# The attention's pass for the largest scores: high part of the queries alone, one shared maximum over the last keys

## Chip, cores and metric

The kernel runs on one core of one Trainium2 chip. The metric is the time of one execution on the device in microseconds; of several executions the median counts.

## The reference, cut to what matters

Two layers of a diffusion backbone over 1024 latent tokens of width 1024, with 256 context tokens. The change lies in layer 0, whose mixer runs grouped-query attention beside a bidirectional mLSTM. The attention has 8 query heads of 64, two key/value heads, 1280 keys (256 of context, 1024 latent):

```python
s = jnp.einsum('bhgtd,bhsd->bhgts', qblk, kt).astype(jnp.float32) * scale
p = jax.nn.softmax(s, axis=-1).astype(vt.dtype)
return jnp.einsum('bhgts,bhsd->bhgtd', p, vt)
```

The output projection, an expert-choice mixture of 16 experts, and a second layer (pooling mixer, 16 experts again) follow.

## The kernel before, in words

Matmuls that need float32 accuracy are made of float32r parts: a value is split into a high part and a low part, each exact in float32r, and a product is the sum of three products of parts.

*Layout.* For a head the queries stand along the free dimension, 1024 of them, in two tiles. QA has the high part of the 64 channels twice (partitions 0 to 63 and 64 to 127). QB has the low part in partitions 0 to 63, zeros below, and in row 64, once it is known, the negated largest score of each query. For the keys, KS has the high part over the low part, and K2 the high part over a row of ones (row 64) and zeros. So QA times KS is the queries' high part times the whole keys, and QB times K2 is the queries' low part times the keys' high part, plus the number in row 64. One product after the other into the same place gives a score with its query's largest score taken off.

*The pass for the largest scores* is `largest(h)`, a generator. For each of 8 tiles of 128 queries it makes three tiles of scores in PSUM (keys 0 to 511, 512 to 1023, 1024 to 1279), each with two matmuls (lines 648 and 649), and VectorE takes the maximum along the keys (line 650): 24 steps per head. At its end VectorE takes the maximum over the three blocks (653), TensorE transposes (655), ScalarE copies (657), the row goes to DRAM from the SP queue (659) and from there into row 64 of QB from the POOL queue (660). `queries(h)` fills QA and QB; ScalarE writes QA, VectorE the low part.

*The pass for the output* is `weighted(h)`: in 20 iterations (two halves of the queries, ten tiles of 128 keys) two matmuls (683, 684) make scores with the keys along the partitions, ScalarE takes the exponential (686) and its high part (57), VectorE the low part (58, for head 7 692 and 693), and three matmuls (695 to 697) add into the output and the sum. 684 is the matmul that reads QB with row 64 filled.

*Order.* `largest(0)` is stepped inside layer 0's projections, five steps of the attention's start per token tile, its score tiles in the projections' PSUM pool `tr` with three places. For heads 0 to 6, while `weighted(h)` runs, `largest(h + 1)` is stepped twice in iterations 0, 1, 2 of each five and once in the two others; one step of the mLSTM follows each five. The mLSTM has 24 steps, so it ends during head 5 or 6. Score tiles of `largest` have two places in PSUM here (`sc`), those of `weighted` two (`se`). The framework decides, when the program is built, in which order each engine's queue holds its instructions, with the program's order as priority; each engine then runs its queue in order, and waits on semaphores.

Of the kernel before, what the change touches and what calls it, by code (L numbers as in the profile page):

```python
# [11 lines left out]
F32 = mybir.dt.float32  # L12
# [6 lines left out]
AX = mybir.AxisListType.X  # L19
PSUM = bass.MemoryType.PSUM  # L20
# [5 lines left out]
NT = 8            # latent token tiles  # L26
NTA = 10          # context + latent token tiles
KB = 8            # blocks of 128 along the model width
# [4 lines left out]
ORDER = (3, 2, 1, 0)      # layer 1's groups of channels, the last ones first  # L33
# [3 lines left out]
def bc(ap, n=128):  # L37
    """rows of a DRAM vector for n partitions"""
    return bass.AP(tensor=ap.tensor, offset=ap.offset, ap=[[0, n]] + [list(e) for e in ap.ap][-1:])


class Kern:
# [5 lines left out]
    # ---------------------------------------------------------------- helpers  # L48
# [6 lines left out]
    def split(self, hi, lo, src):  # L55
        """src = hi + lo, each of them exact in float32r"""
        self.nc.scalar.copy(hi, src)  # L57
        return self.nc.vector.tensor_tensor(lo, src, hi.bitcast(F32), op=ALU.subtract).ins  # L58

    def rstd(self, pool, ss, n, tag, power=False):  # L60
        """1/sqrt(ss/n + eps) of a [p, m] tile of sums: a power on GpSimd, or exp(-ln/2) and one Newton step"""
# [20 lines left out]
    def staged(self, shape, name="raw", slot=None):  # L82
        """one of two 8 KB places for what comes from DRAM, in turns"""
        if slot is None:
            self.turn = 1 - self.turn
            slot = self.turn
        return self.raw.tile(shape, F32, name=name, tag=f"raw{slot}")

    def quarters(self, src):
        """two float32r parts of an 8 KB tile [128, KB, 256], each in two tiles of four blocks"""  # L90
# [8 lines left out]
    def load_half(self, w, k0, c0, n, extra=None):  # L99
        """rows k0*128.. of four blocks and columns c0..c0+n of w; two pairs of blocks, each in two float32r parts"""  # L100
# [15 lines left out]
    def table(self, name):  # L116
        """from here on ScalarE's functions come from this set"""
# [6 lines left out]
    # ---------------------------------------------------------------- constants  # L124
    def consts(self, pool, tmp, psp):
# [9 lines left out]
        # vectors that are wanted along the partitions: rows, then one transpose  # L135
# [28 lines left out]
    def mixer_consts(self, pool, tmp):  # L164
        """masks of the scans' two directions, and the matrix that reverses a chunk"""
# [13 lines left out]
    def choice_consts(self, pool, tmp):  # L179
        """for the choice of tokens: partitions are (token tile, expert)"""  # L180
# [30 lines left out]
    # ---------------------------------------------------------------- adaLN  # L211
    def mod0(self, pool, work, pp, tr, hp):
        """shift and scale of layer 0 for latent and context, as columns"""
# [29 lines left out]
    def mod_steps(self, xp, work, psp):  # L243
        """the other rows of the latent stream's modulation, in small steps: to DRAM, or for a norm's first two to columns"""
# [41 lines left out]
    # ---------------------------------------------------------------- layer 0, norm and projections  # L286
    def norm_transpose(self, xp, hp, sp, psp, srcs, dst, a, s, act=()):
        """two token tiles -> modulated rmsnorm, transposed, in two float32r parts; dst(j) -> (hh, hl) of blocks j, j + 1"""
# [29 lines left out]
    def layer0_proj(self, early):  # L318
# [3 lines left out]
        with ExitStack() as es:  # L322
# [24 lines left out]
            def hb(t, k):  # L347
                """stationary operands of token tile t (two of context, then latent), block k"""
# [8 lines left out]
            # rotary tables times the head norms' weights (q also times the scale of the scores)  # L357
# [20 lines left out]
            def headnorm(ps, nh, which, t, dst):  # L378
                """rmsnorm of nh heads of 64 and the rotation (latent tiles), into dst"""
# [132 lines left out]
    def gates(self, psp, pool):  # L512
        """the scalars of the mLSTM: rows are (chunk, direction, head), time runs along them, reversed for backward"""
# [64 lines left out]
        # M and the weight of the state along the free dimension, in the order of the tokens  # L578
# [7 lines left out]
    # ---------------------------------------------------------------- layer 0, attention and mLSTM  # L586
    def attention_start(self, es, psp):
        """keys and values of both kv heads, and the first head's queries with their largest scores"""
# [30 lines left out]
    def queries(self, h):  # L619
        """queries of head h along the free dimension: the high part twice; the low part over zeros"""  # L620
# [17 lines left out]
    def largest(self, h):  # L638
        """the largest score of each query of head h, negated, as a row of QB"""
        nc, sp = self.nc, self.qs  # L640
        QA, QB = self.Q[h]
        mx = sp.tile([128, NT, 3], F32, name="mx", tag="mx")
        for t in range(NT):
            ts = slice(t * 128, (t + 1) * 128)
            for b, (c0, c1) in enumerate(((0, 512), (512, 1024), (1024, 1280))):
                ps = self.sc[0].tile([128, 512], F32, name=self.sc[1], tag=self.sc[1])
                o = ps[:, :c1 - c0]
                nc.tensor.matmul(o, QA[:, ts], self.KS[h // 4][:, c0:c1], start=True, stop=False)
                nc.tensor.matmul(o, QB[:, ts], self.K2[h // 4][:, c0:c1], start=False, stop=True)
                nc.vector.reduce_max(mx[:, t, b:b + 1], o, axis=AX)  # L650
                yield
# [10 lines left out]
    def mixers(self):  # L662
        tc, nc, I = self.tc, self.nc, self.I
        KS, K2, VA, VL, Q = self.KS, self.K2, self.VA, self.VL, self.Q
        with ExitStack() as es:
# [7 lines left out]
            def weighted(h):  # L673
                """exp(scores - largest), keys along the partitions, times the values; over the sum"""
# [32 lines left out]
            for h in range(8):  # L707
# [4 lines left out]
                for i, _ in enumerate(weighted(h)):  # L712
                    for _ in range(2 if i % 5 < 3 else 1):
                        next(nxt, None)
                    if i % 5 == 4:
                        next(M, None)
# [9 lines left out]
    def mlstm_steps(self, pool, psp):  # L726
        """both scans, the context's two chunks first; a chunk's output when both directions have been there"""
# [12 lines left out]
    def mlstm(self, pool, psp, d, c):  # L740
# [18 lines left out]
        # what both directions share: the keys by position, and keys times queries  # L759
# [59 lines left out]
    def mlstm_out(self, pool, psp, c):  # L819
        """head norm and output gate of a latent chunk, transposed to channels"""  # L820
# [19 lines left out]
    # ---------------------------------------------------------------- second half of a layer: norm, router, choice  # L840
    def norm2_load(self, l, rows, wr, tmp):
        """the vectors of a layer's second half; rows: tiles for its scale and shift"""
# [8 lines left out]
    def norm2_setup(self, l, n2, xt, nj, st, pst, psl):  # L851
        """pools of a layer's second half. The router takes the stream itself: the norm's weight goes into the
        router's, its shift into a constant"""
# [17 lines left out]
    def half(self, t, x1, c):  # L871
        """half of the columns of a token tile of the stream: its squares' sum, and the channels along the partitions"""
# [10 lines left out]
    def logits(self, t, c, start, stop):  # L883
        """the router's product with half of the channels of a token tile"""
# [5 lines left out]
    def norm2(self, t, x1):  # L890
        """x1 of a token tile -> DRAM; 1/rms"""
# [7 lines left out]
    def store(self, dst, t, src, pairs):  # L899
        """a token tile to DRAM, or two of them that lie together"""  # L900
# [5 lines left out]
    def normed(self, t, x1, r):  # L906
        """the modulated norm of a token tile -> DRAM"""
# [18 lines left out]
    def router(self, t, c, r):  # L926
        """the affinities of a token tile, with half c of the channels still to come"""
# [12 lines left out]
    def topk(self, p, pools):  # L940
        """per expert the 128 tokens of largest affinity, the lower token first among equals: each token's slot, or none.
        The 128th largest comes digit by digit, two bits at a time: as floats of one sign order like their bits"""
# [69 lines left out]
        # the affinities in three exact parts  # L1012
# [6 lines left out]
    def wo_piece(self, i):  # L1019
        """a quarter of the output projection: half of the rows, half of the columns"""  # L1020
# [6 lines left out]
    def R(self, i, shape, dt=F32R):  # L1027
        """one of the 8 KB places"""
# [3 lines left out]
    def out0(self):  # L1032
        """output projection of layer 0, residual, then the second half's preparation"""
# [69 lines left out]
    # ---------------------------------------------------------------- experts  # L1103
    def moe(self, l, last=False):
        tc, nc, I = self.tc, self.nc, self.I
        with ExitStack() as es:
# [37 lines left out]
            def turned(src, nm):  # L1144
                """[slot, 1024] -> transposed blocks in two float32r parts"""
# [18 lines left out]
            def choose(e):  # L1164
                """token numbers and gates of an expert's slots, picked by products with ones and zeros"""
# [34 lines left out]
            for e in range(16):  # L1200
# [32 lines left out]
                if e == 15:  # L1233
                    # the stream after 15 experts; the last one's rows come by a product with ones and zeros
# [21 lines left out]
            def rows(t):  # L1256
                """the last expert's rows, onto x in PSUM or in SBUF, in turns"""
# [45 lines left out]
            def scale(x):  # L1303
                """1/rms"""
# [15 lines left out]
    # ---------------------------------------------------------------- layer 1  # L1320
    def w_raw(self, i):
        """a group's columns of layer 1's projection"""
# [4 lines left out]
    def w_normed(self, raw, out, t, engine):  # L1327
        """the norm's weight in w_raw(i); the norm's shift times it, summed over the blocks"""
# [11 lines left out]
    def w_shift(self, s1):  # L1340
        """the shift's way through the weights, one number per channel"""
# [7 lines left out]
    def layer1(self):  # L1349
        tc, nc, I = self.tc, self.nc, self.I  # L1350
        LO = [w // 2 for w in (2, 4, 8, 16)]
        with ExitStack() as es:
# [5 lines left out]
            # 1/count of the clipped windows at both ends  # L1358
# [15 lines left out]
            # the channel scales of the mixer and of its way into the stream  # L1374
# [7 lines left out]
            def invariants():  # L1382
                """1/rms of the tokens along the free axis"""
# [9 lines left out]
            def channels(i, between=iter(())):  # L1393
                """u of a group, its window means minus u, in two parts; the group's weights"""
# [27 lines left out]
                for m in range(2):  # L1422
                    # u with zeros on both sides, then windows of doubling width
# [35 lines left out]
            def done_half():  # L1459
                """the columns of the first two groups, while the last one is under way"""  # L1460
# [143 lines left out]
```

## Time and profile before

| what | us |
|---|---|
| median of 3 runs | 2348.63 |
| lowest, highest run | 2342.78, 2350.05 |
| span of the profiled execution, first to last instruction | 2342.2 |
| the profiled execution's own time beside its span | not shown by any view |
| `largest(0)`, inside the projections | 353 to 379 |
| attention with mLSTM, `weighted` of heads 0 to 7 | 391 to 751 |

The span comes from one profiled execution, the runs from others. Lines named PE are TensorE matmuls, PEld its weight loads, DVE VectorE, ACT ScalarE, POOL GpSimd, SP the sync engine; a q behind the name marks the engine's sequencer, which issues transfers. A duration of a matmul includes its way through the pipeline, so that consecutive ones overlap.

### The profile page before, as it was taken

How to read it: one execution, taken by the hardware profiler on the slowest of the kernel's cores; microseconds unless marked ns; L12 is line 12 of the kernel's file. 1: busy time of each engine (PE TensorE's matmuls, PEld its weight loads, DVE VectorE, ACT ScalarE, POOL GpSimd, SP SyncE). 2: the span in 40 equal slices, each digit the busy share in tenths (PEclk: the TensorE clock that was granted, in tenths of full speed). 3: DMA queues.
4: the chain of work that ended last, by engine and by line, in shares of the span. 5: the costliest groups of instructions: out<-in, count | busy, mean ns of one | idle time of the engine just before them, and what ended most of it. 6: DMA issues, size and time to landing. Idle time of an engine off the chain costs nothing.

```text
span 2342.2 us, 30036 instructions
## 1 busy us (share of the span) xinstructions
PE 2164.1 (92%) x10531; PEld 1729.5 (74%) x10531; DVE 1982.6 (85%) x3075; ACT 1406.1 (60%) x1994; POOL 259.3 (11%) x369
## 2 busy tenths in 40 slices
PE   6889999999998984999999999889749999999997
PEld 3768887787675863788888887578637888888875
DVE  7887754889997548999999998886789999999986
ACT  6413223667785223777777777522337777777774
POOL 0111120000000020000000010550300000000001
PEclk9899999999999996999999999999869999999999
DMA  7576753233423656999999996322849999999974
GB/s 271 197 248 231 257 176 99 66 109 89 111 76 113 226 203 258 355 381 394 380 385 387 380 386 227 99 73 88 335 177 358 389 383 378 391 384 378 394 250 153
DMA packets 206636, 599.42 MB, mean 256 GB/s; under 512 B 16708, under 2 KB 60180, under 8 KB 205460
## 3 DMA queue, kind: packets, MB, share of 16 engines
q1 hardware_dynamic: 168480, 481.81, 54.3%
q0 software_dynamic: 20704, 74.49, 10.9%
q10 hardware_dynamic: 17300, 41.20, 4.9%
q8 instruction: 83, 1.36, 0.2%
q14 instruction: 69, 0.57, 0.1%
HBM read 544.87 MB, written 52.58 MB: 255 GB/s over the span
## 4 chain that ended last, share of the span: by engine, by line
PE 77%; DVE 11%; ACT 4%; DMA 4%; issue 3%; POOL 1%; ACTq 0%; POOLq 0%; DVEq 0%; SPq 0%
PE u L51 6%; PE u L52 6%; PE u L53 6%; PE g L53 5%; PE g L52 5%; PE g L51 5%; PE d L52 5%; PE d L53 5%; PE d L51 5%; PE pp L51 3%; PE pp L52 3%; PE pp L53 3%; PE tr L1151 2%; DVE wl L58 2%; PE y L51 2%
## 5 line engine op out<-in xcount | busy, mean ns | idle before, releaser
L58 DVE TENSOR_TENSOR wl<-R,wh 128x1024 fp32r<-128x1024 f32 x512 | 614.4, 1236 | 39.2 <-ACT wh L57 36.7
L57 ACT CAST wh<-R 128x1024 fp32r<-128x1024 f32 x512 | 534.1, 1052 | 173.1 <-PE d L53 56.5
L58 DVE TENSOR_TENSOR wl<-X,wh 128x1024 fp32r<-128x1024 f32 x178 | 211.0, 1219 | 13.9 <-ACT wh L57 13.1
L57 ACT CAST wh<-X 128x1024 fp32r<-128x1024 f32 x178 | 186.0, 1050 | 54.8 <-PE d L53 22.8
L52 PE MATMUL d<-wl,ah 128*128 128x512 f32 x512 | 203.8, 398 | 5.5 <-DVE wl L58 5.5
L51 PE MATMUL d<-wh,ah 128*128 128x512 f32 x512 | 205.1, 400 | 2.9 <-DVE o L1186 2.9
L51 PE MATMUL g<-wh,xh 128*128 128x512 f32 x512 | 206.1, 402 | 1.5 <-ACT xh L57 1.5
L52 PE MATMUL g<-wl,xh 128*128 128x512 f32 x512 | 203.1, 397 | 1.8 <-DVE wl L58 1.8
L51 PE MATMUL u<-wh,xh 128*128 128x512 f32 x512 | 204.4, 399 | 0.0
L52 PE MATMUL u<-wl,xh 128*128 128x512 f32 x512 | 202.6, 396 | 0.6 <-DVE wl L58 0.6
L53 PE MATMUL g<-wh,xl 128*128 128x512 f32 x512 | 203.2, 397 | 0.0
L53 PE MATMUL d<-wh,al 128*128 128x512 f32 x512 | 202.8, 396 | 0.0
L53 PE MATMUL u<-wh,xl 128*128 128x512 f32 x512 | 202.1, 395 | 0.0
L57 ACT CAST wh<-raw 128x1024 fp32r<-128x1024 f32 (+1 forms) x112 | 115.5, 1037 | 56.8 <-PE pp L53 13.9
L58 DVE TENSOR_TENSOR wl<-raw,wh 128x1024 fp32r<-128x1024 f32 (+1 forms) x112 | 131.7, 1202 | 14.0 <-ACT wh L57 13.0
L686 ACT ACTIVATE e<-se 128x512 f32<-128x512 f32 x160 | 93.3, 595 | 65.2 <-PE se L684 49.9
L52 PEld LDWEIGHTS d<-wl,ah 128*128 128x128 f32 x512 | 96.8, 189 | 29.8 <-DVE wl L58 8.9
L51 PEld LDWEIGHTS d<-wh,ah 128*128 128x128 f32 x512 | 96.9, 189 | 25.1 <-ACT ah L57 3.8
L52 PEld LDWEIGHTS g<-wl,xh 128*128 128x128 f32 x512 | 97.2, 190 | 23.8 <-DVE wl L58 2.7
L51 PEld LDWEIGHTS g<-wh,xh 128*128 128x128 f32 x512 | 97.1, 190 | 23.6 <-ACT xh L57 2.5
L52 PEld LDWEIGHTS u<-wl,xh 128*128 128x128 f32 x512 | 96.4, 188 | 23.2 <-DVE wl L58 1.9
L53 PEld LDWEIGHTS d<-wh,al 128*128 128x128 f32 x512 | 96.8, 189 | 22.7 <-DVE al L58 0.5
(559 smaller groups left out, 4944.9 us busy)
## 6 DMA issues: line engine op xcount, KB each, us to landing
R<-in_w_exp_gate SPq DMA_DIRECT2D x87, 1024.0 KB
R<-in_w_exp_down SPq DMA_DIRECT2D x85, 1024.0 KB
R<-in_w_exp_up SPq DMA_DIRECT2D x79, 1024.0 KB
wm<-in_w_mod POOLq DMA_DIRECT2D x80, 512.0 KB, 5.3
X<-in_w_exp_up SPq DMA_DIRECT2D x33, 1024.0 KB
X<-in_w_exp_down SPq DMA_DIRECT2D x30, 1024.0 KB
X<-in_w_exp_gate SPq DMA_DIRECT2D x26, 1024.0 KB
raw<-in_w_exp_up SPq DMA_DIRECT2D x16, 1024.0 KB
```

The lines of the kernel that those rows point to most:

```text
L51: mm(ps, lh, rh, start=start, stop=False)
L52: mm(ps, lh, rl, start=False, stop=False)
L53: self.mark = mm(ps, ll, rh, start=False, stop=stop).ins
L57: self.nc.scalar.copy(hi, src)
L58: return self.nc.vector.tensor_tensor(lo, src, hi.bitcast(F32), op=ALU.subtract).ins
L686: nc.scalar.activation(e, ps, AF.Exp)
L1151: nc.tensor.transpose(ps[:, j * 128:(j + 1) * 128], src[:, (4 * q + j) * 128:(4 * q + j + 1) * 128], self.idf)
```

## The change

The matmul with the queries' low part is left out of `largest`, so that the number found is the largest product of the high part alone. What is subtracted from a score before the exponential is common to numerator and sum. The first two blocks of keys keep a PSUM tile each per tile of queries. For the last 256 keys, two tiles of queries share one PSUM tile, and one reduction gives both maxima. There are 20 steps per head instead of 24, and `mixers` takes them in another rhythm: two in iteration 0 of each five, one in the four others. The diff also strips comments and docstrings, which is left out here.

```diff
     def largest(self, h):
         nc, sp = self.nc, self.qs
         QA, QB = self.Q[h]
+        KS = self.KS[h // 4]
         mx = sp.tile([128, NT, 3], F32, name="mx", tag="mx")
-        for t in range(NT):
-            ts = slice(t * 128, (t + 1) * 128)
-            for b, (c0, c1) in enumerate(((0, 512), (512, 1024), (1024, 1280))):
-                ps = self.sc[0].tile([128, 512], F32, name=self.sc[1], tag=self.sc[1])
-                o = ps[:, :c1 - c0]
-                nc.tensor.matmul(o, QA[:, ts], self.KS[h // 4][:, c0:c1], start=True, stop=False)
-                nc.tensor.matmul(o, QB[:, ts], self.K2[h // 4][:, c0:c1], start=False, stop=True)
-                nc.vector.reduce_max(mx[:, t, b:b + 1], o, axis=AX)
-                yield
+        PS = lambda: self.sc[0].tile([128, 512], F32, name=self.sc[1], tag=self.sc[1])
+        for t in range(0, NT, 2):
+            for i in range(2):
+                for b in range(2):
+                    ps = PS()
+                    nc.tensor.matmul(ps, QA[:, (t + i) * 128:(t + i + 1) * 128], KS[:, b * 512:(b + 1) * 512],
+                                     start=True, stop=True)
+                    nc.vector.reduce_max(mx[:, t + i, b:b + 1], ps, axis=AX)
+                    yield
+            ps = PS().rearrange("p (i k) -> p i k", i=2)
+            for i in range(2):
+                nc.tensor.matmul(ps[:, i], QA[:, (t + i) * 128:(t + i + 1) * 128], KS[:, 1024:1280], start=True, stop=True)
+            nc.vector.reduce_max(mx[:, t:t + 2, 2], ps, axis=AX)
+            yield
         m8 = sp.tile([128, NT], F32, name="m8", tag="m8")
...
                 for i, _ in enumerate(weighted(h)):
-                    for _ in range(2 if i % 5 < 3 else 1):
+                    for _ in range(2 if i % 5 == 0 else 1):
                         next(nxt, None)
```

## Rows read from the trace of the kernel before

**Rows 1.** The page: span; busy time, share and instructions of two engines.
```profile
span 2342.2 us, 30036 instructions
...
PE 2164.1 (92%) x10531; PEld 1729.5 (74%) x10531; DVE 1982.6 (85%) x3075; ACT 1406.1 (60%) x1994; POOL 259.3 (11%) x369
```

**Rows 2.** Window of `largest(0)`: busy us per engine; then its matmuls by form, 348 to 391.
```profile
353.40:379.30 25.90, 25.90 (x121) 21.16 (x120) 14.34 (x27) 3.76 (x7) 0.00 (x0) 1.00 0.10 38
...
L648 PE MATMUL tr<-KS,QA 128*128 128x512 f32 x16 | 6.5, 406 | 0.0
L649 PE MATMUL tr<-K,QB 128*128 128x512 f32 x16 | 6.3, 394 | 0.0
```

**Rows 3.** Windows by head: PE, PEld, DVE, ACT, POOL busy (count), clock, DMA.
```profile
391.10:435.70 44.60, 41.70 (x200) 30.81 (x199) 36.02 (x72) 31.22 (x59) 2.80 (x9) 0.96 0.38 117
435.70:486.40 50.70, 50.35 (x284) 39.58 (x282) 43.63 (x95) 35.08 (x74) 1.76 (x5) 1.00 0.29 88
486.40:537.70 51.30, 51.18 (x302) 42.26 (x300) 46.09 (x105) 36.96 (x83) 1.85 (x6) 1.00 0.39 113
537.70:582.20 44.50, 43.47 (x233) 33.82 (x231) 41.24 (x100) 31.64 (x74) 1.75 (x5) 1.00 0.29 78
582.20:626.80 44.60, 40.69 (x203) 29.58 (x201) 41.54 (x104) 33.75 (x92) 1.16 (x3) 1.00 0.40 104
626.80:678.70 51.90, 48.85 (x264) 38.40 (x264) 49.33 (x129) 40.25 (x107) 2.13 (x5) 1.00 0.25 74
678.70:715.00 36.30, 33.97 (x155) 24.55 (x152) 33.72 (x64) 32.17 (x62) 0.00 (x0) 1.00 0.36 116
715.00:751.30 36.30, 30.93 (x110) 18.33 (x110) 28.64 (x53) 18.21 (x30) 1.32 (x8) 0.95 0.31 98
```

**Rows 4.** Timeline in head 1: start, duration, instruction; 512 columns, then 256.
```profile
452.02 0.39 PE L648 MATMUL sc<-KS,QA 128*128 128x512 f32 x1
...
452.25 0.39 PE L649 MATMUL sc<-K,QB 128*128 128x512 f32 x1
...
453.00 0.28 PE L648 MATMUL sc<-KS,QA 128*128 128x256 f32 x1
...
453.12 0.28 PE L649 MATMUL sc<-K,QB 128*128 128x256 f32 x1
```

**Rows 5.** VectorE's groups by form, 391 to 751: busy, mean ns, idle before.
```profile
L650 DVE TENSOR_REDUCE mx<-sc 128x1 f32<-128x512 f32 x112 | 75.8, 684 | 6.8 <-PE sc L649 6.2
L650 DVE TENSOR_REDUCE mx<-sc 128x1 f32<-128x256 f32 x56 | 23.2, 415 | 1.7 <-PE sc L649 1.6
...
L653 DVE TENSOR_REDUCE m<-mx 128x8 f32<-128x24 f32 x7 | 1.2, 170 | 0.0
```

**Rows 6.** Timeline at the seventh boundary, from the last reduction on.
```profile
711.25 0.42 DVE L650 TENSOR_REDUCE mx<-sc 128x1 f32<-128x256 f32 x1
...
713.81 0.30 SPq L659 DMA_DIRECT2D md<-mr  x1
...
715.56 0.48 POOL L660 DMA_DIRECT2D QB<-md  x1 [38.53 <-PE se L683]
...
717.65 0.39 PE L683 MATMUL se<-QA,KS 128*128 128x512 f32 x1
...
720.21 0.64 PE L684 MATMUL se<-QB,K 128*128 128x512 f32 x1 [2.17 <-DMA QB<-md]
```

**Rows 7.** TensorE's waits, 391 to 751: us in total, times, longest.
```profile
PE se L684 <- DMA QB<-md: 2.2, 1, 2.2
```

**Rows 8.** Windows in and behind that wait, columns as in rows 3.
```profile
717.50:720.30 2.80, 0.63 (x4) 0.20 (x2) 1.90 (x2) 0.00 (x0) 0.00 (x0) 1.00 0.64 245
720.30:722.00 1.70, 1.70 (x4) 1.04 (x5) 0.43 (x1) 1.09 (x2) 0.00 (x0) 0.54 0.00 0
```

**Rows 9.** Timeline after the stage: the first load of an expert's weights.
```profile
759.35 0.52 SPq L1121 DMA_DIRECT2D R<-in_w_exp_gate  x1
```

## Prediction

> **What bounds the kernel now.** I read the page first: TensorE 92% busy, VectorE 85% [rows 1]. Over a whole program that says little, so I looked up where the edited lines run. `largest` for head 0 runs inside the projections (353 to 379 us). `largest` for heads 1 to 7 runs beside `weighted` of the head before it, from 391 to 715 us; head 7's `weighted` then runs alone to 751. These two places have different limits.
>
> In the first place TensorE is the limit. It is busy 25.9 of 25.9 us, VectorE 14.3, ScalarE 3.8, and the two groups of matmuls of `largest` stand there with no idle time of TensorE ahead of them [rows 2]. A matmul that goes here should come back whole.
>
> In the second place the table by head shows TensorE near 95% and VectorE near 90% [rows 3]. TensorE's busy time is not its occupation: one 512-column matmul lasts 0.39 us in the timeline, but the next starts 0.23 us after it; a 256-column one is followed after 0.12 us [rows 4]. What a removed matmul gives back is the step between starts, at most 0.23 and 0.12. VectorE's instructions don't overlap, so its 41 to 49 us of a 45 to 52 us head are real work. In heads 4 to 6 it is busy 124.6 of 132.8 us, 93.8%; in heads 1 to 3 only 131.0 of 146.5, 89.4%. Heads 4 to 6 carry less mLSTM, so fewer matmuls (203, 264 and 155, against 284, 302 and 233). I read this so: where TensorE is light, VectorE alone sets the pace and loses about 6% to waits; where it is heavy, the two disturb each other and VectorE loses over 10%.
>
> A rule of the Trainium skill (Perfetto Trace Analysis, Identifying the Most-Contended Engine) bears on this: matmul busy time is a poor measure, weight-load busy time a better one, and for VectorE occupancy is the measure. By it VectorE, not TensorE, is the contended engine; the rows agree (weight loads take 29.6 to 42.3 us in the windows of heads 0 to 5, each time less than VectorE's work). It speaks against the change; what it would make of the time is rival B.
>
> **The change, part by part.** *The low-part matmuls.* Per head 16 of 512 columns and 8 of 256 go: 16 x 0.23 + 8 x 0.12 = 4.6 us of TensorE. Eight heads: 37 us. For head 0 all of it counts: **-4.6 us**. For heads 1 to 7 it counts (32 us) only where TensorE sets the pace.
>
> *The shared last maximum.* Per head eight 256-column reductions become four over two rows of 256, one of 512 elements with two results. No row shows that form. It can't be under the 0.684 us of a 512-element reduction with one result, and at worst costs two of 0.415, i.e. 0.83. Several results per partition look free: the reduction of 24 elements to eight results takes 0.170 us [rows 5], and the straight line through 256 and 512 elements (269 ns more for 256 more) gives 0.415 - 232 x 0.00105 = 0.171 for 24. So I take 0.684: 8 x 0.415 - 4 x 0.684 = 0.58 us less VectorE per head; zero is the other bound.
>
> *VectorE's share in heads 1 to 6.* Their 279.3 us hold 255.6 us of VectorE. Less 6 x 0.58 that is 252.1. After the change TensorE has 4.6 us less in each, so heads 1 to 3 should come to resemble heads 4 to 6. At their 93.8%: 252.1 / 0.938 = 268.8, **-10.5 us**. Bounds: at 91.5%, no better than these six together have now, 275.5 (-3.8); at 98%, 257.2 (-22). I take 93.8% because heads of this kernel reach it with TensorE light. Head 0's window holds the start of the stage, which waits on loads; I give it VectorE's saving alone, **-0.6 us**.
>
> *Steps.* Twenty steps instead of 24, taken 6 per 5 iterations of `weighted` instead of 8. The 24th step was taken in iteration 14 and the finish (maximum over blocks, transpose, copy, write to DRAM, load into row 64 of QB) called in iteration 15; now it is called in 16, one iteration later. An iteration lasts 279.3 / 120 = 2.3 us. That chain is long: before head 7 the last reduction starts at 711.25, the write is issued at 713.81, the load at 715.56, and TensorE starts its first product with QB at 720.21, after waiting [rows 6]. This wait is the only one of its kind in the stage [rows 7], so the other six boundaries have some slack, the seventh none. Queued behind the waiting matmul are all later products of TensorE, and ScalarE's exponentials wait for those. I charge the seventh boundary with the full iteration: **+2.3 us**. Against that, spreading the reductions evens VectorE's load; I book nothing for it, the 98% bound holds it.
>
> *Granted clock.* In that wait the row of 717.5 to 720.3 has 0.63 us of TensorE, and in the next 1.7 us the granted clock is 0.54, close to the 1.2 GHz level [rows 8]: 0.8 us lost at each such wait. One is in the time of before already, so the sum has nothing for it.
>
> *Edits at nothing.* `largest` no longer needs QB, which VectorE fills after ScalarE has filled QA; that can bring its first tile forward by one VectorE operation per head, but VectorE, the tighter engine, has other work then. If it has none, the gain is that one operation. No transfer is added or moved past another on SP or POOL, except that the QB load comes later.
>
> *After the stage.* The first expert weights are issued at 759.35, behind the loads of the attention's output [rows 9], so the stream of weights moves with the end of the attention; I pass the gain on whole.
>
> Sum: -4.6 - 10.5 - 0.6 + 2.3 = **-13.4 us**. The trace's execution has a span of 2342.2 us; what lies around it isn't shown, and the fastest run (2342.78) is only 0.6 above the span, the median 2348.63 6.4 above it. I take the difference off the median: 2335.2, say **2335 us**.
>
> **Rivals.** *A, TensorE was the bound in heads 1 to 7 too.* For it: 50.4 of 50.7 and 51.2 of 51.3 us busy in heads 1 and 2. Against: the steps of [rows 4], and heads 4 to 6. Then all 37 us come back: 2311.6.
>
> *B, VectorE is the bound throughout, and what it loses to waits has nothing to do with TensorE.* Then 4.6 us come from head 0's pass and 7 x 0.58 / 0.91 = 4.5 from the reductions, nothing else: 2339.5. For it: in head 5 VectorE is at 95% already. Against: 89% in heads 1 to 3, while TensorE is heavy. The section of the Trainium skill named above leads to this rival.
>
> *C, slower: the row of maxima comes too late at every head.* All seven boundaries then stop TensorE at its first product with QB. Today's stop is 2.6 us from start to start. The other six would pay that, the later iteration (2.3) and the half clock (0.8), 5.7 each, the seventh 2.3: 36.5 us against 15.7 gained, 2369. It decides from a mean of 15.7 / 7 = 2.2 us per boundary, and is slower by over 7 us from 3.3. For it: no slack at the seventh. Against: one stop in seven now, and a delay of 2.3 us alone reaches that mean only where there is no slack anywhere.
>
> **Numbers.** Forecast 0.55, A 0.15, B 0.2, C 0.1. The forecast's own range by its bounds: -3.8 instead of -10.5 gives 2342, -22 gives 2324. A full is 2312, and halfway to it 2323. 8 times in 10: 2319 to 2346, which leaves out the best of A and the worse half of C. About 7 us (0.3%) is what a measurement here can tell from no change. Faster by more: the forecast but its upper end, A, and half of B: 0.75. Within: 0.16. Slower: 0.09.
>
> **What the profile after would show.** Right: `largest` of head 0 has 24 matmuls and the projections' pass is 4 to 5 us shorter; reductions of the shared tile near 0.68 us; heads 1 to 3 with VectorE at 93 to 94% and 2 to 5 us shorter, heads 4 to 6 about 0.6; the stop at the seventh boundary longer, the clock dipping after it. A: every head shorter by 4 us or more. B: heads unchanged but for half a us, VectorE's share unchanged. C: TensorE's waits on the load into QB at most boundaries. The prediction would be wrong most simply if the order written into the queues for the new program is worse or better than the old one at other waits, above all exponentials late for VectorE.

## The result and the profile after

The changed kernel takes 2322.05 us (median of 4 runs, 2320.64 to 2325.28), against 2348.57 for the kernel before (2342.78 to 2350.05): ratio 0.9897, 95% interval 0.9882 to 0.9912. That is 26 us less by these medians, where 13 were forecast. The ratio stands for 24 us (21 to 28), and against the 2345.8 to 2346.7 us that the kernel before took in later runs it is 24 as well.

The page of the changed kernel: its span, and the line of busy times that answers to [rows 1].

```profile
span 2323.5 us, 29647 instructions
...
PE 2133.2 (92%) x10339; PEld 1702.9 (73%) x10339; DVE 1974.5 (85%) x3043; ACT 1407.9 (61%) x1994; POOL 258.1 (11%) x369
```

192 matmuls (the 8 x 24 of the low part) and 32 VectorE instructions are gone. The span fell by 18.7 us, 7.8 less than the medians did: a span lies 1.8 us below the time of its run, so the profiled execution of before was one of 2344.0 us, 4.6 under its median, and the changed kernel's took 2325.28, 3.2 over its own. In the profiles of all kernels below, the stage of the attention starts at 384.6 to 394.4 us; about half of that spread is head 0's pass, the rest lies in the projections ahead of it, where nothing was edited. So lengths of stretches are compared below, not starts.

*Head 0's pass.* From the first transpose of its queries to the first product of `weighted`, in the timeline of the kernel before:

```profile
351.17 0.60 PE L633 MATMUL tr<-idf,qr 128*64 128x128 f32 x4
...
391.13 0.49 PE L683 MATMUL se<-QA,KS 128*128 128x512 f32 x1
```

and of the changed one:

```profile
353.99 0.60 PE L633 MATMUL tr<-idf,qr 128*64 128x128 f32 x4
...
389.13 0.48 PE L690 MATMUL se<-QA,KS 128*128 128x512 f32 x1
```

39.96 against 35.14 us: -4.8.

*The stage by head.* Windows of the changed kernel, each from one head's first product to the next one's, with the columns of [rows 3]:

```profile
389.10:425.10 36.00, 32.51 (x153) 24.23 (x151) 29.10 (x55) 27.09 (x47) 1.38 (x7) 0.95 0.45 136
425.10:473.10 48.00, 46.94 (x263) 36.94 (x264) 44.41 (x96) 36.63 (x80) 2.73 (x7) 1.00 0.34 92
473.10:520.20 47.10, 45.80 (x272) 37.22 (x271) 44.37 (x100) 35.83 (x80) 1.55 (x5) 1.00 0.44 121
520.20:562.50 42.30, 39.42 (x212) 30.29 (x210) 40.12 (x94) 33.15 (x77) 1.79 (x7) 1.00 0.37 92
562.50:612.10 49.60, 41.64 (x195) 31.21 (x194) 44.77 (x108) 36.95 (x99) 1.90 (x5) 0.93 0.35 95
612.10:661.00 48.90, 44.26 (x215) 32.15 (x214) 45.20 (x111) 38.07 (x99) 1.65 (x4) 0.97 0.28 77
661.00:698.20 37.20, 33.70 (x154) 24.11 (x154) 35.57 (x75) 33.43 (x68) 0.49 (x1) 1.00 0.34 111
698.20:735.00 36.80, 30.61 (x112) 18.77 (x110) 31.09 (x56) 20.24 (x32) 1.33 (x8) 0.95 0.33 105
```

Against [rows 3], head 0 lost 8.6 us, heads 1 to 3 2.7, 4.2 and 2.2, head 4 gained 5.0, head 5 lost 3.0, head 6 gained 0.9. Work has moved across the heads' boundaries with the new order of the queues (VectorE's work in head 0's window is 29.1 us where it was 36.0), so single heads can't be compared; the stage can. The sign that the prediction named for heads 1 to 3 (2 to 5 us shorter) came out, the one for heads 4 to 6 (0.6 us each) didn't. To the end of head 7's division it is 345.9 us long, against 360.8 (391.1 to 751.9) before. VectorE's share of it rose from 89 to 91%, in heads 1 to 6 from 91.5 to 93.2% (254.4 of 273.1 us). The two stages in one window each, before's first:

```profile
391.10:751.90 360.80, 341.14 (x1734) 257.33 (x1732) 320.82 (x716) 259.28 (x575) 12.77 (x41) 0.99 0.33 98
...
389.10:735.00 345.90, 314.88 (x1566) 234.93 (x1564) 314.62 (x688) 261.38 (x575) 12.81 (x41) 0.98 0.36 102
```

*The reductions.* VectorE's groups in the stage, columns as in [rows 5]; the second line is the shared form:

```profile
L652 DVE TENSOR_REDUCE mx<-sc 128x1 f32<-128x512 f32 x112 | 75.3, 680 | 1.4 <-PE sc L650 1.3
...
L657 DVE TENSOR_REDUCE mx<-sc 128x2 f32<-128x512 f32 x28 | 19.1, 681 | 0.0
```

The two results per partition cost nothing. The pass takes 94.4 us of VectorE instead of 99.0.

*The seventh boundary.* Timeline of the changed kernel, answering to [rows 6], and its one wait on the load into QB, answering to [rows 7]:

```profile
697.01 0.67 DVE L657 TENSOR_REDUCE mx<-sc 128x2 f32<-128x512 f32 x1
...
699.27 0.30 SPq L666 DMA_DIRECT2D md<-mr  x1
...
701.02 0.48 POOL L667 DMA_DIRECT2D QB<-md  x1 [35.55 <-DMA md<-mr]
...
702.43 0.50 PE L704 MATMUL po<-el,VA 128*128 128x512 f32 x1 [1.41 <-DVE el L58]
702.88 0.70 PE L691 MATMUL se<-QB,K 128*128 128x512 f32 x2
```

```profile
PE se L691 <- DMA QB<-md: 0.6, 1, 0.6
```

From the last reduction to the first product with QB 5.9 us pass, where it was 9.0 before, and TensorE has other products in between, the last of which waits 1.41 us for VectorE. The stop was forecast to grow by 2.3 us; it shrank from 2.2 to 0.6.

### The profile page after: what moved, and what is told of

Same layout as the page of the kernel before. It is cut to its first block, busy times and chain, and to the rows that moved or that the text cites. A ratio compares the mean times of both kernels' runs of the same rounds, so it can differ in the third digit from the quotient of the medians.

```text
span 2323.5 us, 29647 instructions
## 1 busy us (share of the span) xinstructions
PE 2133.2 (92%) x10339; PEld 1702.9 (73%) x10339; DVE 1974.5 (85%) x3043; ACT 1407.9 (61%) x1994; POOL 258.1 (11%) x369
## 4 chain that ended last, share of the span: by engine, by line
PE 56%; DVE 8%; issue 2%; ACT 2%; POOL 1%; DMA 1%; ACTq 0%; POOLq 0%; DVEq 0%; SPq 0%
PE u L51 6%; PE u L52 6%; PE u L53 6%; PE g L53 5%; PE g L52 5%; PE g L51 5%; PE d L52 5%; PE d L53 5%; PE d L51 5%; PE tr L1158 2%; DVE wl L58 2%; PE y L51 2%; PE y L53 2%; PE y L52 1%; DVE tjunk L978 1%
## 5 line engine op out<-in xcount | busy, mean ns | idle before, releaser
L57 ACT CAST wh<-X 128x1024 fp32r<-128x1024 f32 x178 | 186.0, 1050 | 54.8 <-PE d L53 23.2
L52 PEld LDWEIGHTS u<-wl,xh 128*128 128x128 f32 x512 | 96.4, 188 | 23.2 <-DVE wl L58 1.9
```

Of the source, the lines that this page charges most:

```text
L52: mm(ps, lh, rl, start=False, stop=False)
```

## Experiments

Four theories stood behind the expectations: P, the prediction's (VectorE sets the pace, and loses less to waits when TensorE is lighter); A, TensorE is the bound; V, the shared maximum gives the gain; S, the rhythm of the steps gives it. "Stage" is the stretch from the first product of `weighted` to the end of head 7's division, one window each, with the columns of [rows 3].

**The kernel before once more** (no edit).

> The kernel before once more, unchanged: ratio 1. Its profile shows which stretch of the program takes another time in another execution; the span of the first profile (2342.2 us) and the median of its runs (2348.6) differ by 6.4 us. If the projections' loads make the difference, it lies ahead of 350 us; if the attention does, between 391 and 751.

2346.35 us, ratio 0.9998 (0.9989 to 1.0008). Its stage:

```profile
390.40:753.40 363.00, 342.53 (x1734) 259.19 (x1732) 320.99 (x716) 259.27 (x575) 12.78 (x41) 0.99 0.34 98
```

The stage repeats within 2.2 us (360.8, 363.0); what is smaller than that is not read from one profile.

**The low part left out, nothing else.**

```diff
-                nc.tensor.matmul(o, QA[:, ts], self.KS[h // 4][:, c0:c1], start=True, stop=False)
-                nc.tensor.matmul(o, QB[:, ts], self.K2[h // 4][:, c0:c1], start=False, stop=True)
+                nc.tensor.matmul(o, QA[:, ts], self.KS[h // 4][:, c0:c1], start=True, stop=True)
```

> The kernel before with the low-part matmul of the pass left out, and nothing else: 24 steps, the old rhythm, eight separate reductions of 256. What is subtracted from the scores is then the largest product of the queries' high part. Theory P (VectorE sets the pace, and a lighter TensorE lets it lose less to waits): this alone gives most of the change, -18 to -24 us, since only 4.6 us of VectorE and the rhythm are missing. Theory A (TensorE was the bound): -37 us. Theory V (the shared maximum gives it, TensorE's relief is hidden in heads 1 to 7): -5 us, head 0's pass alone. Theory S (the steps' rhythm gives it): -5 us as well.

2331.06 us, ratio 0.9929 (0.9912 to 0.9947): -15 us by medians, less than P's range, whose lower end (-18) lies inside the interval of -12 to -21.

```profile
389.70:739.60 349.90, 317.46 (x1566) 232.45 (x1563) 315.91 (x716) 260.81 (x575) 12.81 (x41) 0.97 0.36 101
```

The stage is 11 to 13 us shorter. 32 us of TensorE's steps were taken out of it, so nearly two thirds of them didn't come back.

**The low part put back into the changed kernel** (shared maximum and new rhythm alone).

```diff
                     nc.tensor.matmul(ps, QA[:, (t + i) * 128:(t + i + 1) * 128], KS[:, b * 512:(b + 1) * 512],
-                                     start=True, stop=True)
+                                     start=True, stop=False)
+                    nc.tensor.matmul(ps, QB[:, (t + i) * 128:(t + i + 1) * 128], K2[:, b * 512:(b + 1) * 512],
+                                     start=False, stop=True)
```

The two 256-column matmuls of a shared tile get theirs in the same way.

> The changed kernel with the low-part matmuls put back: shared maximum over the last 256 keys, 20 steps, new rhythm, TensorE's work as before. P: -3 to -6 us (VectorE's 4.6 us over its share of 0.9), nothing in head 0's pass. A: 0 to -2 us. V: -20 us or more. S: -10 us or more.

2346.98 us, ratio 1.0002 (0.9993 to 1.0011): nothing, as A has it.

```profile
392.70:756.90 364.20, 345.19 (x1734) 256.69 (x1732) 317.91 (x688) 260.88 (x575) 12.78 (x41) 0.99 0.34 97
```

The same 4.6 us of reductions that are saved here buy nothing while TensorE carries the low part. V falls.

**Head 0 alone.**

```diff
-                nc.tensor.matmul(o, QA[:, ts], self.KS[h // 4][:, c0:c1], start=True, stop=False)
-                nc.tensor.matmul(o, QB[:, ts], self.K2[h // 4][:, c0:c1], start=False, stop=True)
+                nc.tensor.matmul(o, QA[:, ts], self.KS[h // 4][:, c0:c1], start=True, stop=h == 0)
+                if h:
+                    nc.tensor.matmul(o, QB[:, ts], self.K2[h // 4][:, c0:c1], start=False, stop=True)
```

> The kernel before, with the low-part matmul left out for head 0 alone, whose pass runs inside the projections. All theories: -4.6 us, 24 matmuls at their steps of 0.23 and 0.12 us, with the rest of the program later by nothing. If the order of the queues behind it matters, the time differs from that by several us with the stage from 391 to 751 us longer or shorter.

2343.58 us, ratio 0.9988 (0.9980 to 0.9997), which is -0.7 to -4.7 us. The pass in its timeline:

```profile
350.38 0.60 PE L633 MATMUL tr<-idf,qr 128*64 128x128 f32 x4
...
385.65 0.49 PE L684 MATMUL se<-QA,KS 128*128 128x512 f32 x1
```

35.27 us against 39.96: -4.7, by the profile as forecast. The medians show 2.6, at the edge of what they can tell. Its stage is 362.8 us, like before.

**The old rhythm in the changed kernel.**

```diff
-                    for _ in range(2 if i % 5 == 0 else 1):
+                    for _ in range(2 if i % 5 < 3 else 1):
```

> The changed kernel with the rhythm of before: two steps in iterations 0 to 2 of each five, so that the 20 steps end in iteration 12. P: within 4 us of the changed kernel, the row of maxima earlier and VectorE's load less even. S: slower than the changed kernel by 8 us or more. If the later row cost the changed kernel what was forecast (2.3 us at the seventh boundary), this one is 2 us faster there.

2322.95 us, ratio 0.9903 (0.9888 to 0.9917), stage 346.3 us: the changed kernel's time. S falls; that the row of maxima is asked for in iteration 12 instead of 16, four earlier, is worth nothing either.

**The row of maxima late.**

```diff
-                    for _ in range(2 if i % 5 == 0 else 1):
+                    for _ in range(2 if i == 0 else 1):
```

> The changed kernel with one step per iteration, two only in iteration 0: the 20 steps end in iteration 18 and the row of maxima is asked for in 19 instead of 16, three iterations or some 6.5 us later. Rival C (the row is the critical thing at the heads' boundaries): TensorE stops at the first product with QB at all seven boundaries, 3 to 6 us each, 20 to 40 us slower than the changed kernel, with the granted clock dipping behind each stop. P with cover (other work stands between): under 10 us slower.

2346.15 us, ratio 0.9996 (0.9987 to 1.0004): 24 us slower than the changed kernel, its gain gone. Windows of heads 5, 6 and 7:

```profile
613.20:667.10 53.90, 48.56 (x235) 36.15 (x235) 48.91 (x121) 38.49 (x102) 0.73 (x4) 0.94 0.25 70
667.10:710.60 43.50, 37.77 (x142) 25.78 (x140) 37.83 (x68) 35.60 (x67) 1.40 (x2) 0.88 0.37 121
710.60:753.00 42.40, 30.93 (x106) 17.80 (x104) 27.43 (x54) 17.24 (x30) 1.32 (x8) 0.88 0.20 63
```

and TensorE's only wait on the load:

```profile
PE se L691 <- DMA QB<-md: 5.0, 1, 5.0
```

These three heads have 16.9 of the stage's 19.6 us more (139.8 against 122.9). P's "under 10 us" fails. Rival C's size was right, its form wasn't: the loss is not a stop at each of seven boundaries, but lies in the last three windows, with a granted clock of 0.88 in two of them. That little mLSTM is left there to stand between is a likely reason; no run shows it, and the stop at the load is 5.0 us of the 19.6.

**More VectorE, before and after.** In the kernel before, each 256-element reduction of heads 1 to 7 twice; in the changed one, two of 256 more per shared tile; 56 of 0.415 us in both. The line that makes the tile `dm` is left out here.

```diff
+                if h and b == 2:
+                    nc.vector.reduce_max(dm[:, t:t + 1], o, axis=AX)
```

```diff
+            if h:
+                for i in range(2):
+                    nc.vector.reduce_max(dm[:, t + i:t + i + 1], ps[:, i], axis=AX)
```

> The kernel before with each 256-element reduction of heads 1 to 7 made a second time into a tile that nothing reads: 56 x 0.415 = 23.2 us more VectorE, nothing else. If VectorE sets the pace (P, B): +23 to +26 us. If TensorE does (A): +5 to +12 us, since VectorE has 40 us of idle time in the stage of 360.

> The changed kernel with two more reductions of 256 elements per shared tile in heads 1 to 7, into a tile that nothing reads: 23.2 us more VectorE, as in the run beside it. P: +23 to +26 us against the changed kernel, and more than the same load costs the kernel before, if TensorE had a part in the pace there. B (VectorE throughout, before too): the same price in both. A: the change moved the bound from TensorE to VectorE, so this one pays 20 us or more and the other half of that at most.

Before: 2353.45 us, ratio 1.0028 (1.0018 to 1.0038), +7 us for the added reductions. After: 2344.31 us, ratio 0.9993 (0.9979 to 1.0007), +22 us against the changed kernel (its profiled execution took 2351.28). The two stages, before's first:

```profile
394.40:764.20 369.80, 343.07 (x1734) 257.41 (x1731) 335.54 (x772) 261.29 (x575) 12.75 (x41) 0.99 0.33 96
```

```profile
389.40:758.50 369.10, 324.92 (x1566) 237.48 (x1563) 333.36 (x744) 263.17 (x575) 12.79 (x41) 0.96 0.34 96
```

The same load costs the stage 7 to 9 us before the change and 23.2 after it. What was added is less than 23.2 us, though, as VectorE's timeline shows in the second of these runs:

```profile
503.64 0.68 DVE L658 TENSOR_REDUCE mx<-sc 128x2 f32<-128x512 f32 x1
504.24 0.75 DVE L661 TENSOR_REDUCE dm<-sc 128x1 f32<-128x256 f32 x2
504.90 0.68 DVE L58 TENSOR_TENSOR el<-e,eh 128x512 fp32r<-128x512 f32 x1
```

An instruction recorded with 0.68 us is followed after 0.60, and two of 0.415 take 0.66: VectorE's records overlap by 0.08 us. 56 steps of 0.33 are 18.5 us. So since the change the stage pays the whole load and nearly 5 us besides; before it pays less than half. Part of the 5 us may be TensorE's clock: the same 1566 matmuls are busy 324.9 us here and 314.9 in the changed kernel, with a granted clock of 0.96 for 0.98, while in the kernel before it is 0.99 with the load and without. Even if all 10 us were the clock's, 13 would be left to VectorE's load. Since the change VectorE sets the pace; before it didn't.

**TensorE's time put back without QB.** Each high-part matmul of heads 1 to 7 twice, the second over the first; one of the two edits:

```diff
+                    if h:
+                        nc.tensor.matmul(ps, QA[:, (t + i) * 128:(t + i + 1) * 128], KS[:, b * 512:(b + 1) * 512],
+                                         start=True, stop=True)
```

> The changed kernel with each high-part matmul of the pass made twice into the same place in heads 1 to 7 (the second writes over the first): TensorE's 32 us are back, with no operand of QB, no other shape and no other step. If TensorE's time is the reason, +15 to +20 us in the stage, as in the run with the low part put back (364 against 346 us). If it was the product with QB that hurt (its wait for VectorE's copy, another weight), 0 to +6 us.

2344.22 us, ratio 0.9998 (0.9989 to 1.0006), +22 us against the changed kernel.

```profile
387.80:752.40 364.60, 344.51 (x1734) 257.22 (x1731) 318.35 (x688) 260.74 (x575) 12.73 (x41) 0.99 0.34 97
```

The stage is that of the run with the low part put back (364.2). It was TensorE's time that cost, not the operand QB.

**Less VectorE, by way of GpSimd.** In the kernel before and in the changed one:

```diff
-            nc.vector.tensor_tensor(E, E, self.mk[d][:, None, :].to_broadcast([128, 4, 128]), op=ALU.add)
+            nc.gpsimd.tensor_tensor(E, E, self.mk[d][:, None, :].to_broadcast([128, 4, 128]), op=ALU.add)
-            nc.vector.tensor_tensor(wi, wi, qT, op=ALU.mult)
+            nc.gpsimd.tensor_tensor(wi, wi, qT, op=ALU.mult)
```

and in a third kernel the scaling of `v` and of `ob` besides.

> The kernel before with two VectorE operations of the mLSTM's chunks (the mask added to the decay rows, the queries scaled by the state's weight; 16 each of 0.68 us) given to GpSimd, where a 128x512 product takes 1.3 us: 21.8 us less VectorE in the stage. From the runs with more VectorE (+6.8 us for 23.2 us before, some +22 us after): if TensorE held the pace before, this gives -7 us at most; if VectorE did, -20 us. GpSimd has room (13 of 346 us busy), but the longer way of a chunk could cost a few us.

> The changed kernel with the same two operations given to GpSimd. If VectorE alone sets the pace since the change, -15 to -22 us against the changed kernel, some 2302 us. If TensorE and ScalarE stand close behind, or a chunk's longer way through GpSimd counts, under 8 us. The difference to the run beside it, taken against its own base, tells how the change moved the bound.

> As the run before, and the scaling of the values (18 of 0.69 us) and of the output gate (8 of 0.68 us) given to GpSimd too: 39.7 us less VectorE in all, GpSimd some 77 us. If VectorE is still the bound after the first step, a further -10 to -16 us; if another engine has taken over (ScalarE has 261 us of work, TensorE some 265 us by its steps), 0 to -5 us.

2387.1 us (1.0173, 1.0159 to 1.0187), 2348.82 us (1.0016, 1.0006 to 1.0026) and 2337.03 us (0.9963, 0.9950 to 0.9976): all three slower than their base, by 41, 27 and 15 us. For the first two that is the opposite of what was expected; the third is 12 us faster than the second, which lies in its -10 to -16. In the second one, VectorE's splits and ScalarE's two waits on GpSimd:

```profile
L58 DVE TENSOR_TENSOR el<-e,eh 128x512 fp32r<-128x512 f32 x140 | 105.5, 761 | 17.4 <-ACT eh L57 17.2
```

```profile
ACT E L787 <- POOL E L785: 19.0, 8, 3.5
ACT E L787 <- POOL v L757: 13.7, 6, 3.7
```

ScalarE runs the mLSTM's exponentials (E) and the attention's in one queue. With the mask on GpSimd, which itself waits for loads in its own queue, ScalarE stood 32.7 us at E in all, and the attention's exponentials behind it. In the third it stood there 16.4 us, so that its step of 12 us may be the shorter wait as well as the lighter VectorE. These runs say nothing on VectorE's pace: they took away a load and put in a wait.

## Why the prediction was right, and where it was off

*TensorE as the limit around head 0's pass* held: -4.6 forecast, -4.8 and -4.7 in two profiles.

*The shared reduction* held as a duration: 0.684 us taken, 0.681 measured. Its saving did not. The prediction takes VectorE's instructions as not overlapping and counts durations; by the steps of 0.60 and 0.33 us a head saves 8 x 0.33 - 4 x 0.60 = 0.24 us of VectorE, not 0.58. Between the run without the low part and the changed kernel VectorE's busy time in the stage fell by 1.3 us (315.9 to 314.6).

*Heads 1 to 7* are where the forecast fell short: 8.8 us (10.5, 0.6 and -2.3), and the stage gave 14.9 against the first profile of before, 17.1 against the second. Its terms were mis-sized, and the first for a wrong reason. VectorE's share in heads 1 to 6 came out as taken (93.2% for 93.8%), but these windows gave 6.2 us instead of 10.5, and the term was blind to work that moved across the boundary from head 0, which gave 8.6 instead of 0.6. And the charge of 2.3 us for a later row was not paid: that stop shrank, and the run with the row four iterations earlier takes the same time.

The wrong reason is the step that read heads 4 to 6 as "VectorE alone sets the pace". Before the change a load of 18.5 us on VectorE cost the stage 7 to 9 us, and the shared reductions alone bought nothing (364.2 against 360.8 and 363.0). Two limits, the longer one deciding, order the runs better than shares do:

| kernel | VectorE's limit | TensorE's limit | stage measured |
|---|---|---|---|
| before | 350 | 362 | 360.8, 363.0 |
| low part out | 350 | under 346 | 349.9 |
| shared maximum, low part kept | 346 | 362 | 364.2 |
| changed | 346 | under 346 | 345.9 |
| changed, old rhythm | 346 | under 346 | 346.3 |
| changed, TensorE's time put back | 346 | 362 | 364.6 |
| before, VectorE +23.2 | 373 | 362 | 369.8 |
| changed, VectorE +23.2 | 369 | under 346 | 369.1 |

Three numbers are set from runs: 362 is the mean of the two profiles of before, 350 and 346 are the stages of the two kernels in which TensorE is light; 373 and 369 are these and 23.2, the sum of durations; with the steps' 18.5 they are 368 and 364. All lengths agree within 4 us, within 5 by steps; "under 346" was not measured. By this TensorE was the bound of the stage, as rival A had it, with VectorE 12 us behind. No run loads ScalarE, which is busy some 260 us of the stage, so a part of its own in the pace is not excluded. The section of the Trainium skill that the prediction weighed (Perfetto Trace Analysis, Identifying the Most-Contended Engine) names the engine of the highest occupancy, here VectorE (89% of the stage, TensorE's weight loads 71%). For the kernel before the measurement says otherwise, for the changed one it agrees. Of TensorE's 32 us, 12 came back until VectorE's limit was met. The shared maximum, worth nothing alone, took another 4 us off the stage (349.9 to 345.9, or 346.3 in the old rhythm), 8 or 9 by medians, where the intervals touch. That is more than the 1.3 us of VectorE's time that it saves; it also takes five score tiles for two tiles of queries instead of six, and no run tells which of these counts. So the gain is neither A's 37 nor B's 9: with head 0's 4.8 the table gives 4.8 + 16 = 21, the lower end of the interval of 21 to 28. Where in the program the medians' remaining 3 to 5 us lie was not found.

*What was luck:* the gain is nearly twice the forecast, and it lies in the range because the range went halfway to rival A, whose reading of the bound fits the kernel before better than the forecast's own.

*The gain is passed on whole:* held. From the end of the stage to the end of the span 1590.3 and 1588.6 us before, 1588.5 after.

*Left open:* what makes TensorE's limit 362 us. Counted by the steps of [rows 4], its matmuls take some 315 us of the stage (1024 of 512 columns at 0.23, 112 of 256 at 0.12, and 598 of 128 or 129 columns, transposes among them, which follow one another after 0.11 us in the timeline; an estimate from these). That leaves some 45 us. The waits of its weight loads sum to 53 us in the stage before, 30 of it for ScalarE and 18 for VectorE, the largest of them:

```profile
PEld se L683 <- ACT e L686: 13.6, 27, 0.9
PEld po L695 <- ACT eh L57: 7.0, 24, 0.7
PEld po L697 <- DVE el L58: 6.6, 15, 1.1
```

So the limit holds waits for the two other engines besides TensorE's own work. No run took them away one by one.

## What to carry to other kernels

Where two engines are both about 90% busy, their shares don't tell which one sets the pace: load one of them by a known amount, counted from start to start, and see whether the stage pays all of it, a third or nothing. An edit that buys nothing alone (the shared maximum) can buy something behind another one that moves the bound. Moving work to an idle engine adds a wait to every in-order queue that uses the result; look at what else stands in that queue first.

## What the runs showed of the hardware that was not expected

With two operations of 128x512 on GpSimd per chunk and direction, VectorE's splits of the same shape took 0.761 us on average instead of 0.680, though no operand is shared; the reductions, which read PSUM, stayed at 0.68. By the timeline 110 of the splits run beside no such operation of GpSimd and take 0.674 us; the 30 that meet one take 1.04 on average, up to 1.76, as here:

```profile
511.94 1.74 POOL L785 TENSOR_TENSOR E<-E,mk 128x512 f32<-128x512 f32 x1
...
513.05 1.17 DVE L58 TENSOR_TENSOR el<-e,eh 128x512 fp32r<-128x512 f32 x1
```

GpSimd's own two operations took 1.61 and 1.46 us there, where products of that size took 1.3 us later in the changed kernel:

```profile
L785 POOL TENSOR_TENSOR E<-E,mk 128x512 f32<-128x512 f32 x16 | 25.8, 1613 | 12.9 <-DMA E<-MW 12.1 <-PE se L691 0.4 <-DVE dn L800 0.2
L789 POOL TENSOR_TENSOR wi<-wi,qT 128x512 f32<-128x512 f32 x16 | 23.3, 1458 | 139.5 <-DMA wi<-MW 99.0 <-DVE C L821 20.2 <-PE mp L816 16.5
```

So both engines run slower beside each other; 140 splits at 0.08 us are 11 of the 22 us that were to be saved.
